# Low parts of projection weights: a ScalarE negation and an accumulating DMA in place of a subtraction

## The chip, the cores and the metric

One core of a Trainium2 chip runs the whole kernel. The metric is the time of one execution on the device in microseconds; a kernel's time is the median over its runs.

## The reference, cut to what matters

The kernel computes a trunk of two layers on 512 tokens of width 1024, all in float32: an S5 state-space mixer, a SwiGLU feed-forward block (FFN), a sparse attention with a lightning indexer (DSA), and a second FFN.

```python
def s5_mixer(u, ..., w_glu):
    ...
    y = jax.nn.gelu(y).astype(u.dtype)
    val, gate = jnp.split(y @ w_glu, 2, axis=-1)      # w_glu: 1024 x 2048
    return val * jax.nn.sigmoid(gate)

def dsa_mixer(h, w_in, q_gain, k_gain, w_o, cos, sin, topk):
    proj = h @ w_in                                   # w_in: 1024 x 3656
    q, k, v, qi, ki, wi = jnp.split(proj, cuts, axis=-1)
    ...                                               # QK-norm, rotary
    # per block of 128 queries
    score = jnp.einsum('bqhk,bqh->bqk', jax.nn.relu(s_idx), wb)   # 8 index heads
    _, sel = lax.top_k(score, topk)                   # 256 keys of each query
    ...                                               # 16 heads attend to the selected keys
    return out @ w_o
```

## The kernel before, in words

Every float32 product with a weight is made of three products in TensorE's faster type fp32r: a weight block w is split into a high part (w rounded to fp32r) and a low part (w minus the high part), the activations are split in the same way, and high x high, high x low and low x high are summed in PSUM (`mm3` L271 to L274 for the mixer and the FFNs, `project` L1016 to L1030 for the attention's projections). `wblock` (L254 to L268) brings a block of up to 128 x 1024 weights in: a DMA on SyncE's queue (SP, L262) fills `w_raw`, ScalarE (ACT) copies it into `w_hi` with rounding (L263), and the low part is subtracted on VectorE (DVE, L265) or, where a caller hands an engine in, on GpSimd (POOL, L267). There are two buffers of `w_raw`, three of `w_hi` and three of `w_lo`.

Who calls it, in the program's order:

- The S5 layer. While VectorE still builds the state-space operators and TensorE runs the scan, `refill` (L815) fetches 11 blocks of `w_glu` of 512 to 1024 columns for partial sums of the GLU projection, with which `glu_parts` fills the gaps of TensorE. After the scan, `glu_sum` (L844) adds what is missing in 16 blocks of 128 to 768 columns. Their low parts come from VectorE.
- The attention. `weights` (L1011) fetches the columns that a projection needs, in two or three blocks, and their low parts come from GpSimd: five blocks for the index heads (`index_heads`), eight for the values (`values`, four head groups) and four per head group for the queries and keys (`queries_keys`, s = 0 to 3), 29 in all. Queries and keys of head group 0, the index scores (`score`, L1119 and L1121 on VectorE), the choice of the 256 keys (`select`, MAX8 L1133 and MATCH_REPLACE L1134 on VectorE) and the values stand before the first attention scores (`scores`, L1203 and L1204); the head groups 1 to 3 are projected while the group before them attends.
- The two FFNs and the output projection take 152 further blocks, with their low parts on VectorE.

GpSimd also does small steps of the norms of heads (`head_norm`, `hn_ms`, `hn_pw` and the factor `kf`, `fk` or `nsq`), memsets and the causal masks. A tile scheduler sets the order of the instructions on every engine from the order in which the kernel is written and from the buffers; each engine runs its own list in order, and semaphores tie the lists together.

Of the kernel before, what the change touches and what calls it, by code (L numbers as in the profile page):

```python
# [15 lines left out]
AF = mybir.ActivationFunctionType  # L16
ALU = mybir.AluOpType
# [3 lines left out]
P = 128  # L21
D = 1024
# [32 lines left out]
HD = 64  # L55
# [150 lines left out]
class Trunk:  # L206
# [47 lines left out]
    def wblock(self, src, nk, cols, lo_engine=None):  # L254

        nc = self.nc
        raw_t = self.wp.tile([P, KT * P], F32, name="w_raw", bufs=2)
        hi_t = self.wp.tile([P, KT * P], F32R, name="w_hi", bufs=3)
        lo_t = self.wp.tile([P, KT * P], F32R, name="w_lo", bufs=3)
        raw, hi, lo = (t[:, : nk * cols] for t in (raw_t, hi_t, lo_t))  # L260
        v = "p (k c) -> p k c"
        nc.sync.dma_start(out=raw.rearrange(v, k=nk), in_=src)  # L262
        nc.scalar.activation(hi, raw, AF.Copy)  # L263
        if lo_engine is None:
            nc.vector.tensor_tensor(lo, raw, hi, op=ALU.subtract)  # L265
        else:
            lo_engine.tensor_tensor(lo, raw, hi, op=ALU.subtract)  # L267
        return hi.rearrange(v, k=nk), lo.rearrange(v, k=nk)  # L268
# [98 lines left out]
    def s5(self, gain_row, x_ap, lre, lim, ldt, b_re, b_im, c_re, c_im, d_ap, w_glu):  # L367
        nc, tc = self.nc, self.tc
        V, PL, AC, PE = nc.vector, nc.gpsimd, nc.scalar, nc.tensor
        ident = self.ident  # L370
        wg = w_glu.rearrange("(k p) f -> p k f", p=P)
# [37 lines left out]
        def load_x(j):  # L409
            for e in range(2):  # L410
# [8 lines left out]
                          in_=gain_row.rearrange("(o d) -> o d", o=1).to_broadcast([P, D]))  # L419
# [383 lines left out]
        cuts = [u for u in range(UN) for _ in range(GLU_BLOCKS[u])]  # L803
        cut.update(zip(order, cuts))
        groups, n = [], 0
        while n < len(order):
            m = n + 1
# [3 lines left out]
            n = m  # L811
# [3 lines left out]
        def refill(ahead):  # L815
            while fetched[0] < min(len(groups), done[0] + ahead):
                n, m = groups[fetched[0]]
                fetched[0] += 1
                d, i = order[m - 1]
                whi, wlo = self.wblock(wg[:, 0 : cuts[n], i * D + d * P : i * D + (d + m - n) * P], cuts[n], (m - n) * P)  # L820
                for b in range(n, m):
                    c = slice((m - 1 - b) * P, (m - b) * P)
                    ready[b] = whi[:, :, c], wlo[:, :, c]
# [18 lines left out]
                yield  # L842

        def glu_sum(d, i, k0, k1):  # L844
            whi, wlo = self.wblock(wg[:, k0:k1, i * D + d * P : i * D + (d + 1) * P], k1 - k0, P)
            pt = self.acc()
            for k in range(k0, k1):
                self.mm3(pt, whi[:, k - k0], wlo[:, k - k0], y[k], k == k0, k == k1 - 1)
            return pt
# [40 lines left out]
        for u in range(UN):  # L890
# [30 lines left out]
            if more:  # L921
                ES[u + 1] = turns_out(u + 1, E[u + 1])
            refill(3 if u else 2)
            filler(GLU_BLOCKS[u] * u - sum(f))
        manual.close()
# [14 lines left out]
        for d in range(KT):  # L940
            ps = []
            for i in (1, 0):
                ps.append(glu_sum(d, i, cut[d, i], KT))
            sg = self.tmp("A", "sg")
            vl = self.tmp("B", "vl")
            V.tensor_tensor(sg, ps[0], part[d][:, 1], op=ALU.add)
            AC.activation(sg, sg, AF.Sigmoid)
            V.tensor_tensor(vl, ps[1], part[d][:, 0], op=ALU.add)
            V.tensor_tensor(vl, vl, sg, op=ALU.mult)
            V.tensor_tensor(self.x[d], self.x[d], vl, op=ALU.add)  # L950
# [14 lines left out]
    def dsa(self, gain, w_in, qg, kg, w_o, rope_ap):  # L965
        nc, tc = self.nc, self.tc
        V, PL, AC, PE = nc.vector, nc.gpsimd, nc.scalar, nc.tensor
        win = w_in.rearrange("(k p) f -> p k f", p=P)
# [10 lines left out]
        for i, g in ((1, qg), (2, kg)):  # L979
            gbt = sp.tile([P, HD], F32, name=f"rope_g{i}")  # L980
            nc.sync.dma_start(out=gbt, in_=g.rearrange("(o d) -> o d", o=1).to_broadcast([P, HD]))
            for dst, src in ((slice(0, HD), slice(0, HD)), (slice(HD, HD + H), slice(H, HD)),
                             (slice(HD + H, 2 * HD), slice(0, H))):
                n = dst.stop - dst.start
# [23 lines left out]
        ki = self.slot("a12", [P, 2, S], "ki", F32R)  # L1008
        PL.memset(ki[HD:, 1].bitcast(F32), 0.0)

        def weights(c0, n):  # L1011
            nk = min(KT, KT * P // n)
            out = []
            for k0 in range(0, KT, nk):
                m = min(nk, KT - k0)
                whi, wlo = self.wblock(win[:, k0 : k0 + m, c0 : c0 + n], m, n, PL)  # L1016
                out += [(whi[:, j], wlo[:, j]) for j in range(m)]
            return out

        def project(w, t, n):  # L1020

            pt = self.acc(proj_bank[0])
            ts = slice(t * P, (t + 1) * P)
            for k, (whi, wlo) in enumerate(w):
                for i, (l, ww) in enumerate(((0, whi), (1, whi), (0, wlo))):
                    PE.matmul(pt[:, :n], lhsT=h[k][:, l, ts], rhs=ww, start=(k == 0 and i == 0),  # L1026
                              stop=(k == KT - 1 and i == 2))
                if k == KT // 2 - 1:
                    yield
            return pt  # L1030
# [8 lines left out]
        def head_norm(src, nh, t, out, scale):  # L1039

            sqv = self.tmp("B", "hn_sq")[:, : nh * HD].rearrange("p (h d) -> p h d", d=HD)
            ms = sp.tile([P, 4], F32, name="hn_ms", bufs=2)
            for i in range(nh):
                AC.activation(sqv[:, i], src[:, i], AF.Square, accum_out=ms[:, i : i + 1])
            PL.tensor_scalar(ms[:, :nh], ms[:, :nh], r2[:, t : t + 1], EPS, op0=ALU.mult, op1=ALU.add)
            pw = sp.tile([P, 4], F32, name="hn_pw", bufs=2)
            PL.tensor_tensor(pw[:, :nh], ms[:, :nh], self.mhalf[:, :nh], op=ALU.pow)
            PL.tensor_scalar(out, pw[:, :nh], rt[:, t : t + 1], scale, op0=ALU.mult, op1=ALU.mult)

        def hv(ap, nh):  # L1050
            return ap[:, : nh * HD].rearrange("p (h d) -> p h d", d=HD)

        def rope(src, tab, t, nh):
            ab = self.tmp("A", "rope_ab")
            ro = sp.tile([P, 4 * HD], F32, name="ro", bufs=3)
            self.rope(hv(ro, nh), src, tab, t, nh, hv(ab, nh), hv(ab[:, S // 2 :], nh))
            return ro
# [81 lines left out]
        def values(s):  # L1139
            w = weights(2 * D + s * 4 * HD, 4 * HD)  # L1140
            for t in range(TB):
                pt = whole(project(w, t, 4 * HD))
                AC.activation(vv[t][:, s * 4 * HD : (s + 1) * 4 * HD], pt[:, : 4 * HD], AF.Copy, scale=rt[:, t : t + 1])
                yield
# [4 lines left out]
        def flush():  # L1149
            while late:  # L1150
                late.pop()()

        def queries_keys(s):

            q, k = ([self.slot(f"a{s % 2 * 5 + 2 * i + e}", [P, 2, S], f"{nm}{s}{e}", F32R) for e in range(2)]
                    for i, nm in enumerate(("q", "k")))
            kl = [self.slot(t, [P, 2, S], f"kl{s}{e}", F32R)
                  for e, t in enumerate((f"a{s % 2 * 5 + 4}", ("a10", "a11", "a12", "a15")[s]))]
            for e in range(2):
                PL.memset(kl[e][half[1 - e]].bitcast(F32), 0.0)  # L1160
            qk[s] = q, k, kl
            for j in range(2 * TB):
                t, isq = j % TB, j // TB
                if t == 0:
                    w = weights((1 - isq) * D + s * 4 * HD, 4 * HD)
                pt = yield from project(w, t, 4 * HD)
                if isq:
                    head_norm(hv(pt, 4), 4, t, nsq[:, t, s * 4 : s * 4 + 4], -(HD**-0.5))
                    ro = rope(hv(pt, 4), qtab, t, 4)
                    nxt = partial(put_q, q, ro, t)  # L1170
                else:
                    fk = sp.tile([P, 4], F32, name="fk", bufs=2)
                    head_norm(hv(pt, 4), 4, t, fk, 1.0)
                    ro = rope(hv(pt, 4), ktab, t, 4)
                    V.tensor_tensor(hv(ro, 4), hv(ro, 4), fk.unsqueeze(2).to_broadcast([P, 4, HD]), op=ALU.mult)
                    nxt = partial(put_k, k, kl, ro, t)
                flush()
                late.append(nxt)
                yield
# [102 lines left out]
        proj_bank = [None]  # L1282
        index_heads()
        mix(queries_keys(0), score(), 2, 3)
        flush()
        mix((None for s in range(4) for _ in values(s)), select(), 1, 3)
# [78 lines left out]
```

## Time and profile before

| | |
|---|---|
| median of 3 runs | 1295.48 us (1294.7 to 1298.88) |
| the profiled execution, its own time | 1299.89 us |
| its span | 1298.2 us |
| mean granted TensorE clock | 0.99 of full speed |
| S5 layer with its GLU | about 0 to 235 us of the span |
| attention up to its first scores | about 590 to 721 us |
| DMA traffic | 108.65 MB, 84 GB/s in the mean |

In the rows below, PE is TensorE's matmuls, PEld its weight loads, DVE VectorE, ACT ScalarE, POOL GpSimd and SP SyncE. Times are microseconds of the profiled execution unless ns is named. A row of the view by stretches gives the stretch, its length and each engine's busy time in it (with the count of instructions), then the granted clock, the busy share of the 16 DMA engines and GB/s.

### The profile page before, as it was taken

How to read it: one execution, taken by the hardware profiler on the slowest of the kernel's cores; microseconds unless marked ns; L12 is line 12 of the kernel's file. 1: busy time of each engine (PE TensorE's matmuls, PEld its weight loads, DVE VectorE, ACT ScalarE, POOL GpSimd, SP SyncE). 2: the span in 40 equal slices, each digit the busy share in tenths (PEclk: the TensorE clock that was granted, in tenths of full speed). 3: DMA queues.
4: the chain of work that ended last, by engine and by line, in shares of the span. 5: the costliest groups of instructions: out<-in, count | busy, mean ns of one | idle time of the engine just before them, and what ended most of it. 6: DMA issues, size and time to landing. Idle time of an engine off the chain costs nothing.

```text
span 1298.2 us, 17961 instructions
## 1 busy us (share of the span) xinstructions
PE 1223.8 (94%) x6796; PEld 1048.7 (81%) x6796; DVE 769.0 (59%) x1546; ACT 541.9 (42%) x1224; POOL 150.5 (12%) x177
## 2 busy tenths in 40 slices
PE   2569999999999999999989799999999999999998
PEld 1457878888888888888989799998888888888887
DVE  7999958654444443335899977775754444443221
ACT  5645536433333322223563678875533333332221
POOL 2000000000000000005744354520000000000000
PEclk9979999999999999999999899999999999999999
DMA  5101223333333333332213111111333333333341
GB/s 139 54 19 52 71 84 114 104 98 97 97 98 98 98 92 99 94 105 71 92 52 98 49 50 34 42 30 53 106 112 95 96 96 95 97 93 101 108 118 46
DMA packets 189894, 108.65 MB, mean 84 GB/s; under 512 B 7224, under 2 KB 188560, under 8 KB 189744
## 3 DMA queue, kind: packets, MB, share of 16 engines
q1 hardware_dynamic: 189424, 107.35, 28.4%
q8 instruction: 53, 0.87, 0.3%
q14 instruction: 33, 0.27, 0.1%
q10 hardware_dynamic: 384, 0.16, 0.1%
HBM read 103.04 MB, written 2.10 MB: 81 GB/s over the span
## 4 chain that ended last, share of the span: by engine, by line
PE 75%; DVE 8%; ACT 1%; issue 1%; DMA 0%; POOL 0%; ACTq 0%; DVEq 0%; POOLq 0%
PE acc L272 21%; PE acc L273 21%; PE acc L274 21%; PE acc L1026 7%; PE acc L1231 2%; DVE mask L1134 2%; DVE m L1133 2%; PE tr L1220 1%; DVE mask L1121 1%; PE lg L1204 1%; DVE pe L1207 1%; PE lg L1203 1%; PE tr L1063 0%; DVE kl L1081 0%; ACT pe L1210 0%
## 5 line engine op out<-in xcount | busy, mean ns | idle before, releaser
L263 ACT ACTIVATE w_hi<-w_raw 128x1024 fp32r<-128x1024 f32 (+5 forms) x208 | 199.9, 963 | 508.2 <-PE acc L273 461.1
L265 DVE TENSOR_TENSOR w_lo<-w_raw,w_hi 128x1024 fp32r<-128x1024 f32 (+6 forms) x179 | 194.2, 1085 | 146.5 <-ACT w_hi L263 145.4
L272 PE MATMUL acc<-h,w_hi 128*128 128x512 f32 x704 | 274.5, 390 | 0.0
L274 PE MATMUL acc<-h,w_lo 128*128 128x512 f32 x704 | 273.9, 389 | 0.0
L273 PE MATMUL acc<-h,w_hi 128*128 128x512 f32 x704 | 273.7, 389 | 0.0
L1026 PE MATMUL acc<-w_hi,h 128*128 128x256 f32 (+1 forms) x896 | 175.6, 293 | 0.8 <-ACT h L284 0.8
L272 PEld LDWEIGHTS acc<-h,w_hi 128*128 128x128 f32 x704 | 132.1, 188 | 28.0 <-issue 0.5
L274 PEld LDWEIGHTS acc<-h,w_lo 128*128 128x128 f32 x704 | 132.1, 188 | 27.6
L273 PEld LDWEIGHTS acc<-h,w_hi 128*128 128x128 f32 x704 | 132.1, 188 | 27.5 <-issue 0.5
L1026 PEld LDWEIGHTS acc<-w_hi,h 128*128 128x128 f32 x896 | 142.1, 193 | 1.4 <-ACT h L284 1.0
L1026 PE MATMUL acc<-w_lo,h 128*128 128x256 f32 (+1 forms) x448 | 127.3, 289 | 0.3 <-POOL w_lo L267 0.3
L339 DVE TENSOR_TENSOR u<-acc,rinv 128x512 f32<-128x512 f32 x44 | 30.4, 691 | 132.4 <-PE acc L274 132.4
L272 PE MATMUL acc<-f,w_hi 128*128 128x512 f32 x272 | 106.4, 391 | 0.0
L274 PE MATMUL acc<-f,w_lo 128*128 128x512 f32 x272 | 105.9, 389 | 0.0
L273 PE MATMUL acc<-f,w_hi 128*128 128x512 f32 x272 | 105.8, 389 | 0.0
L1026 PEld LDWEIGHTS acc<-w_lo,h 128*128 128x128 f32 x448 | 85.5, 193 | 0.8 <-POOL w_lo L267 0.5
L336 DVE TENSOR_TENSOR g<-acc,rinv 128x512 f32<-128x512 f32 x44 | 30.4, 691 | 85.3 <-PE acc L274 85.1
L267 POOL TENSOR_TENSOR w_lo<-w_raw,w_hi 128x1024 fp32r<-128x1024 f32 (+2 forms) x29 | 69.5, 2407 | 47.6 <-ACT w_hi L263 46.8
L274 PEld LDWEIGHTS acc<-f,w_lo 128*128 128x128 f32 x272 | 51.0, 188 | 10.8
L273 PEld LDWEIGHTS acc<-f,w_hi 128*128 128x128 f32 x272 | 51.1, 188 | 10.4
L272 PEld LDWEIGHTS acc<-f,w_hi 128*128 128x128 f32 x272 | 51.1, 188 | 10.4
L272 PE MATMUL acc<-y,w_hi 128*128 128x512 f32 x128 | 51.9, 414 | 1.7 <-ACT y L796 1.1
(288 smaller groups left out, 1979.4 us busy)
## 6 DMA issues: line engine op xcount, KB each, us to landing
w_raw<-in_ffn_w_gate_up_dram SPq DMA_DIRECT2D x88, 512.0 KB, 3.7
w_raw<-in_ffn_w_down_dram SPq DMA_DIRECT2D x32, 448.0 KB, 3.5
w_raw<-in_dsa_w_in_dram SPq DMA_DIRECT2D x26, 512.0 KB, 3.4
w_raw<-in_ffn_w_down_dram SPq DMA_DIRECT2D x16, 512.0 KB, 3.7
w_raw<-in_dsa_w_o_dram SPq DMA_DIRECT2D x16, 256.0 KB, 2.9
w_raw<-in_s_w_glu_dram SPq DMA_DIRECT2D x6, 384.0 KB, 3.3
xc<-in_x_dram SPq DMA_DIRECT2D x8, 256.0 KB, 8.9
xr<-in_x_dram SPq DMA_DIRECT2D x4, 512.0 KB, 3.7
```

The costliest lines, as they stand in the source:

```text
L263: nc.scalar.activation(hi, raw, AF.Copy)
L265: nc.vector.tensor_tensor(lo, raw, hi, op=ALU.subtract)
L267: lo_engine.tensor_tensor(lo, raw, hi, op=ALU.subtract)
L272: mm(out, lhsT=whi, rhs=xx[:, 0], start=start, stop=False)
L273: mm(out, lhsT=whi, rhs=xx[:, 1], start=False, stop=False)
L274: mm(out, lhsT=wlo, rhs=xx[:, 0], start=False, stop=stop)
L336: nc.vector.tensor_tensor(g, ps[0], rinv, op=ALU.mult)
L339: nc.vector.tensor_tensor(u, ps[1], rinv, op=ALU.mult)
L1026: PE.matmul(pt[:, :n], lhsT=h[k][:, l, ts], rhs=ww, start=(k == 0 and i == 0), stop=(k == KT - 1 and i == 2))
L1133: V.max(m8, sc)
L1134: V.match_replace(out=sc, in_to_replace=m8, in_values=sc, imm_value=GONE)
L1231: PE.matmul(po[s, b][:, i * HD : (i + 1) * HD], lhsT=pT[:, j * P : (j + 1) * P], rhs=vv[j][:, (s * 4 + i) * HD : (s * 4 + i + 1) * HD], st ...
```

## The change

A third way to make the low part. With `"dma"` in the place of the engine, ScalarE writes minus the high part into `w_lo`, and a DMA from GpSimd's queue reads the weights a second time from HBM and adds them to it. `refill`, `glu_sum`, the index heads, the values and the queries and keys of head group 0 take it: 27 blocks whose low parts were VectorE's, and 17 that were GpSimd's. The 12 blocks of the head groups 1 to 3 stay on GpSimd, those of the FFNs and of the output projection on VectorE. Lines behind L264 have three more in the changed kernel.

```diff
@@ wblock
         nc.sync.dma_start(out=raw.rearrange(v, k=nk), in_=src)
         nc.scalar.activation(hi, raw, AF.Copy)
-        if lo_engine is None:
+        if lo_engine == "dma":
+            nc.scalar.activation(lo, hi, AF.Copy, scale=-1.0)
+            nc.gpsimd.dma_start(out=lo.rearrange(v, k=nk), in_=src, accum_op=ALU.add)
+        elif lo_engine is None:
             nc.vector.tensor_tensor(lo, raw, hi, op=ALU.subtract)
@@ refill
-                whi, wlo = self.wblock(wg[:, 0 : cuts[n], i * D + d * P : i * D + (d + m - n) * P], cuts[n], (m - n) * P)
+                whi, wlo = self.wblock(wg[:, 0 : cuts[n], i * D + d * P : i * D + (d + m - n) * P], cuts[n], (m - n) * P, "dma")
@@ glu_sum
-            whi, wlo = self.wblock(wg[:, k0:k1, i * D + d * P : i * D + (d + 1) * P], k1 - k0, P)
+            whi, wlo = self.wblock(wg[:, k0:k1, i * D + d * P : i * D + (d + 1) * P], k1 - k0, P, "dma")
@@ dsa
-        def weights(c0, n):
+        def weights(c0, n, lo="dma"):
...
-                whi, wlo = self.wblock(win[:, k0 : k0 + m, c0 : c0 + n], m, n, PL)
+                whi, wlo = self.wblock(win[:, k0 : k0 + m, c0 : c0 + n], m, n, lo)
@@ queries_keys
-                    w = weights((1 - isq) * D + s * 4 * HD, 4 * HD)
+                    w = weights((1 - isq) * D + s * 4 * HD, 4 * HD, PL if s else "dma")
```

The scheduler moves instructions with it. GpSimd's list between the last index heads and the first keys of head group 0, before (`hn_ms`, `hn_pw` and `kf`, `fk` are the steps of the head norms, `kl` a low part of the keys, cleared):

```order
L1048 TENSOR_SCALAR kf<-hn_pw,rt 128x1
L267 TENSOR_TENSOR w_lo<-w_raw,w_hi 128x1024 x2
L1045 TENSOR_SCALAR hn_ms<-hn_ms,r_4748 128x1
L1160 MEMSET kl_7849 64x1024
L1047 TENSOR_TENSOR hn_pw<-hn_ms,mhalf 128x1
L267 TENSOR_TENSOR w_lo<-w_raw,w_hi 128x1024
L1048 TENSOR_SCALAR kf<-hn_pw,rt 128x1
L1045 TENSOR_SCALAR hn_ms<-hn_ms,r_4748 128x4
```

And there in the changed kernel:

```order
L1051 TENSOR_SCALAR kf<-hn_pw,rt 128x1
L266 DMA w_lo<-in_dsa_w_in_dram 128x4x256 x2
L1048 TENSOR_SCALAR hn_ms<-hn_ms,r_4775 128x1
L1050 TENSOR_TENSOR hn_pw<-hn_ms,mhalf 128x1
L1051 TENSOR_SCALAR kf<-hn_pw,rt 128x1
L1163 MEMSET kl_7893 64x1024
L1048 TENSOR_SCALAR hn_ms<-hn_ms,r_4775 128x4
```

The subtractions are gone from GpSimd's list; in their place stand the issues of two DMAs, ahead of the same small steps.

TensorE's list in the values of head group 2, before (`w_hi_6052` and `w_lo_6053` are the first block of the pair, `w_hi_6058` and `w_lo_6059` the second, `acc1_6063` the sum of the first 128 tokens, `acc1_6133` that of the third):

```order
L1026 MATMUL acc1_6133<-w_lo_6053,h1_4676 128x256
L1026 MATMUL acc1_6133<-w_hi_6052,h2_4682 128x256 x2
L1026 MATMUL acc1_6133<-w_lo_6053,h2_4682 128x256
L1026 MATMUL acc1_6133<-w_hi_6052,h3_4688 128x256 x2
L1026 MATMUL acc1_6063<-w_lo_6059,h4_4694 128x256
L1026 MATMUL acc1_6063<-w_hi_6058,h5_4700 128x256 x2
L1026 MATMUL acc1_6063<-w_lo_6059,h5_4700 128x256
```

And in the changed kernel (first block `w_hi_6092` and `w_lo_6093`, second `w_hi_6099` and `w_lo_6100`; `acc1_6105` belongs to the first tokens, `acc0_6211` to the fourth; L1206 and L1207 are the first attention scores):

```order
L1029 MATMUL acc0_6211<-w_lo_6093,h3_4715 128x256
L1029 MATMUL acc0_6211<-w_hi_6099,h4_4721 128x256 x2
L1206 MATMUL lg_6403<-k00_5203,q00_5201 128x128
L1207 MATMUL lg_6403<-kl00_5205,q00_5201 128x128
L1206 MATMUL lg_6412<-k01_5204,q01_5202 128x128
L1029 MATMUL acc1_6105<-w_lo_6100,h4_4721 128x256
L1029 MATMUL acc1_6105<-w_hi_6099,h5_4727 128x256 x2
```

Before, the low part of the second block is first used when the first block has served not quite three of the four groups of tokens; now it is when it has served all four, and the first attention scores, which stood behind the values of all head groups, stand there too.

ScalarE's list at the start of the GLU sums, before (`xk` are the transposed inputs, `sg` the gate):

```order
L938 ACTIVATE xk_1956<-tr 128x512
L263 ACTIVATE w_hi<-w_raw 128x256
L263 ACTIVATE w_hi<-w_raw 128x384
L947 ACT_TABLE_LOAD
L947 ACTIVATE sg<-sg 128x512
L938 ACTIVATE xk_1963<-tr 128x512
```

And in the changed kernel:

```order
L941 ACTIVATE xk_1967<-tr 128x512
L263 ACTIVATE w_hi<-w_raw 128x256
L263 ACTIVATE w_hi<-w_raw 128x384
L265 ACTIVATE w_lo<-w_hi 128x256
L950 ACT_TABLE_LOAD
L950 ACTIVATE sg<-sg 128x512
L265 ACTIVATE w_lo<-w_hi 128x384
L941 ACTIVATE xk_1974<-tr 128x512
```

The negation of a block stands behind its high part, sometimes with other work of ScalarE between the two.

## Rows read from the trace of the kernel before

**Rows 1.** The page: engines' busy times and shares; the chain by engine.

```profile
PE 1223.8 (94%) x6796; PEld 1048.7 (81%) x6796; DVE 769.0 (59%) x1546; ACT 541.9 (42%) x1224; POOL 150.5 (12%) x177
...
PE 75%; DVE 8%; ACT 1%; issue 1%; DMA 0%; POOL 0%; ACTq 0%; DVEq 0%; POOLq 0%
```

**Rows 2.** Stretches: S5 layer, GLU sums, attention up to its first scores.

```profile
0.00:50.00 50.00, 16.34 (x107) 13.87 (x107) 40.32 (x187) 33.87 (x85) 7.46 (x17) 1.00 0.43 110
50.00:100.00 50.00, 34.58 (x282) 28.78 (x282) 49.26 (x96) 21.82 (x52) 0.23 (x2) 0.86 0.11 29
100.00:150.00 50.00, 48.23 (x346) 39.45 (x347) 47.74 (x87) 24.65 (x51) 0.34 (x3) 1.00 0.21 57
200.00:255.00 55.00, 55.00 (x253) 45.46 (x252) 42.48 (x66) 27.71 (x43) 1.93 (x1) 1.00 0.40 117
...
640.00:755.00 115.00, 102.01 (x777) 98.46 (x776) 110.61 (x279) 66.11 (x214) 57.90 (x53) 0.96 0.21 65
644.00:721.00 77.00, 68.92 (x529) 66.92 (x528) 74.53 (x170) 40.51 (x113) 41.21 (x32) 0.96 0.24 76
...
645.00:655.00 10.00, 7.39 (x55) 7.01 (x54) 9.77 (x18) 5.82 (x29) 6.28 (x7) 0.95 0.35 107
```

**Rows 3.** Timeline from 644 to 653 us, in part, of POOL, DVE and PE.

```profile
644.07 4.94 POOL L267 TENSOR_TENSOR w_lo<-w_raw,w_hi 128x1024 fp32r<-128x1024 f32 x2
644.46 2.29 DVE L963 TENSOR_TENSOR ro<-rope_ab 128x256 f32<-128x256 f32 x1
646.67 2.62 DVE L1121 SCALAR_TENSOR_TENSOR mask<-pe,wi,mask 128x256 f32<-128x256 f32 x1
649.10 0.57 POOL L1045 TENSOR_SCALAR hn_ms<-hn_ms,r 128x4 f32<-128x4 f32 x1
...
652.86 0.41 PE L1063 MATMUL tr<-ident,ro 128*128 128x128 f32 x2 [2.51 <-DVE kl L1081]
```

**Rows 4.** VectorE's groups, 630 to 720 us, then single lines: ns min/median/max.

```profile
L1121 DVE SCALAR_TENSOR_TENSOR mask<-pe,wi,mask 128x256 f32<-128x256 f32 (+2 forms) x21 | 18.8, 897 | 0.2
L963 DVE TENSOR_TENSOR ro<-rope_ab 128x256 f32<-128x256 f32 (+1 forms) x10 | 9.7, 969 | 0.2
...
L1121 DVE SCALAR_TENSOR_TENSOR mask<-pe,wi,mask x21: 469/619/2617, 637.0 to 688.0; 128x256 f32<-128x256 f32 x7, 128x384 f32<-128x384 f32 x7, 128x512 f32<-128x512 f32 x7
...
L963 DVE TENSOR_TENSOR ro<-rope_ab x10: 226/422/2622, 629.3 to 670.9; 128x256 f32<-128x256 f32 x9, 128x64 f32<-128x64 f32 x1
...
L1136 DVE TENSOR_SCALAR mask<-mask x3: 349/428/2343, 692.8 to 755.1; 128x256 f32<-128x256 f32 x1, 128x384 f32<-128x384 f32 x1, 128x512 f32<-128x512 f32 x1
...
L1119 DVE TENSOR_SCALAR mask<-pe,wi x3: 411/479/1743, 635.2 to 673.3; 128x256 f32<-128x256 f32 x1, 128x384 f32<-128x384 f32 x1, 128x512 f32<-128x512 f32 x1
```

**Rows 5.** The chain that ended last, 640 to 725 us, in part.

```profile
682.32 2.57 DVE mask L1121
...
692.90 2.26 DVE mask L1136
```

**Rows 6.** VectorE's low parts in the S5 layer: three up to 100 us, first and last.

```profile
37.81 0.69 DVE L265 TENSOR_TENSOR w_lo<-w_raw,w_hi 128x512 fp32r<-128x512 f32 x1 [0.80 <-ACT w_hi L263]
...
48.41 0.95 DVE L265 TENSOR_TENSOR w_lo<-w_raw,w_hi 128x768 fp32r<-128x768 f32 x1
```

**Rows 7.** ScalarE's high parts by shape, 30 to 260 us: busy us, mean ns.

```profile
L263 ACT ACTIVATE w_hi<-w_raw 128x1024 fp32r<-128x1024 f32 x8 | 8.4, 1057 | 16.1 <-PE acc L273 10.2 <-DMA w_raw<-in_ffn_w_gate_up_dram 5.9
...
L263 ACT ACTIVATE w_hi<-w_raw 128x640 fp32r<-128x640 f32 x6 | 4.4, 738 | 6.4 <-DMA w_raw<-in_s_w_glu_dram 3.6 <-PE acc L273 2.9
```

**Rows 8.** DMA issues: count, KB each, median us from issue to landing.

```profile
w_raw<-in_dsa_w_in_dram SPq DMA_DIRECT2D x26, 512.0 KB, 3.4
...
w_raw<-in_s_w_glu_dram SPq DMA_DIRECT2D x5, 256.0 KB, 2.6
```

**Rows 9.** VectorE's low parts of the last twelve GLU sums, first and last.

```profile
198.59 0.55 DVE L265 TENSOR_TENSOR w_lo<-w_raw,w_hi 128x384 fp32r<-128x384 f32 x1
...
227.91 0.95 DVE L265 TENSOR_TENSOR w_lo<-w_raw,w_hi 128x768 fp32r<-128x768 f32 x1
```

## The prediction

> **What bounds the kernel now.** I read the page first. TensorE is busy 94% of the span and the chain of waits is 75% TensorE, 8% VectorE [rows 1]. So an instruction taken from another engine counts only where TensorE waits, and I looked for those places with the view by stretches. There are two that the change touches.
>
> In the S5 layer VectorE builds operators and is busy for 49.26 of the 50 us from 50 to 100, while TensorE idles 15.4; from 100 on TensorE is busy for 48.23 of 50, and over the GLU sums for all of it [rows 2]. In the attention, from 644 to 721 us, VectorE is busy for 74.53 of 77 us, TensorE idles 8.1 and its clock is granted at 0.96, which takes 68.92 x 0.04 = 2.8 more; over the wider stretch from 640 to 755 it idles 13.0 and loses 4.1 at the same clock [rows 2]. The first score of the attention waits there for VectorE's choice of keys.
>
> The timeline shows why VectorE is late in the second place. While GpSimd subtracts two low parts (4.94 us), a VectorE sum of two SBUF tiles takes 2.29 us and the next instruction, with two such inputs as well, 2.62; TensorE then stands for 2.51 until VectorE gives it `kl` [rows 3]. The same lines take 0.42 and 0.62 in the median [rows 4]. Against the medians the 21 L1121 lose 21 x (0.897 - 0.619) = 5.8 us, the ten L963 10 x (0.969 - 0.422) = 5.5, the first L1136 2.34 - 0.35 = 2.0 and the first L1119 1.74 - 0.48 = 1.3: 14.6 us between 630 and 720. Two of these stand in the chain itself, with 2.57 and 2.26 us [rows 5]. Some 11.6 of the 14.6 start behind 644, seven instructions from the 2.29 at 644.46 to the 2.26 at 692.90.
>
> **The change part by part.**
>
> *S5 layer, VectorE's 27 subtractions go.* Only three stand where TensorE idles, 0.69, 0.95 and 0.95 us at 37.8 to 49.4 [rows 6]; the other 24 run while TensorE is saturated and are worth nothing. That is 2.6 us off a VectorE that sets the pace there. Bounds 0 and 4 (the clock, 0.86 in that stretch, could come up sooner); I take **-2.5**.
>
> *Attention, 17 of GpSimd's subtractions go* (17 of the 19 up to 721 us). VectorE gets its 14.6 us back. It can turn into time only up to what TensorE waits: 8.1 + 2.8 = 10.9 us from 644 to 721, and 17.1 to 755. The 3 us before 644 and part of the wait that is one of TensorE's own order bring nothing. Below, 4 (what stands in the chain: 2.57 - 0.75 and 2.26 - 0.35); above, 14. I take **-8**, two thirds of the waits: VectorE is 97% busy, so nearly all of the 11.6 shifts its later work, and the first scores now stand ahead of the last values, which gives TensorE something to do during the choice of keys.
>
> *ScalarE negates 44 blocks*, at 1.06 us for 1024 columns and 0.74 for 640 [rows 7], 17 x 1.0 + 27 x 0.7 = 36 us in all. It is busy for 40.51 of 77 and 27.71 of 55 us in those stretches [rows 2], so this lies beside other work; what it costs is lateness of the low part, counted next.
>
> *44 accumulating DMAs.* No row shows one. Below, it costs what a plain load costs, 3.4 us for 512 KB and 2.6 for 256 [rows 8]; above, three of them in a row (read the weights, read the tile, write it), 10.2 and 8.6 for the 288 KB of a mean GLU block (at some 2.85 each). Two 512 KB blocks take a share of 0.35 of 16 engines over 10 us [rows 2], so one pass takes 1.75. I take a load, one pass more and an issue of GpSimd like its small steps (0.57 [rows 3]): 3.4 + 1.75 + 0.6, rounded to 6 us, and 2.85 + 1.0 + 0.6 = 4.5 for the GLU. By a sentence of its own: the Trainium skill, "DMA: Bandwidth & Descriptors", section "Anatomy of one DMA — SWDGE (gpsimd) path", fits a plain DMA of GpSimd's queue as 2.0 us plus its bytes over 436e3 per us, an estimate of 3.2 for 512 KB; by it the low part would be earlier than I count, and the trace has no such DMA.
>
> Does TensorE wait for them? A buffer of `w_lo` is held from ScalarE's write to TensorE's last use, and there are three. In the GLU sums the last twelve blocks [rows 9] have 576 columns in the mean, 13.5 matmuls at 55.00/253 = 0.217 us [rows 2], 2.9 us of TensorE each. High part 0.7, negation 0.7, DMA t, use 2.9: three buffers keep pace if 4.3 + t is at most 3 x 2.9, so up to **t = 4.4**. At 4.5 the stall is nothing, at 8.6 it is (4.3 + 8.6)/3 - 2.9 = 1.4 per block, 17 us over twelve. In the attention a block serves 48 matmuls of some 0.12 us, 5.8 us, and 1.05 + 1.05 + t + 5.8 within 17.4 allows up to t = 9.5; the new order of TensorE's list, all four groups of tokens on the first block of a pair, covers one such block. The 11 blocks of the partial sums are spread over 100 us. I take **+1.5** for starts (the first index heads, the first GLU sums), bounds 0 and 21.
>
> *GpSimd's queue.* The small steps of the head norms stand behind DMAs that wait for ScalarE; before, they stood behind 4.9 us of subtractions, so nothing is added. *SyncE* issues the same loads; `w_raw` comes free after ScalarE instead of after the subtraction, 2.4 us sooner, hidden. *HBM* carries the weights of 44 blocks twice, some 16 MB; DMA shares of 0.24 and 0.40 [rows 2] leave room.
>
> Sum: -2.5 - 8 + 1.5 = **-9**. The profiled execution took 1299.89, so it would take 1290.9; it stands 4.4 above the median of the runs, 1295.48, on which the forecast is **1286.5**.
>
> **The rivals.**
>
> *The low parts come late* (slower). An accumulating DMA really takes three passes one after another. It decides at t = 4.4 us in the GLU sums: at 8.6 TensorE loses 17 there. In the attention at 10.2 the cycle is 18.1 against 17.4, 0.2 for each of 17 blocks, 4 in all, and the late values and queries give back half of the 8. 1295.5 + 17 + 4 - 4 - 1 is some **1311**; at t = 7 in the GLU, (4.3 + 7)/3 - 2.9 = 0.9, 10 us, and some **1300**. For it: no row shows such a DMA, and the GLU has the shortest blocks. Against it: the engines are idle for more than half of the time.
>
> *VectorE's gain is hidden* (same). TensorE's waits from 644 to 721 come from its own order (its list places a projection behind transposes that need VectorE's whole rotary chain), so the gain is the 4 us of the chain, the S5 part moves into TensorE's next wait, and 2 to 3 us of late low parts cancel it: **1294**.
>
> *GpSimd still holds VectorE* (faster by less). GpSimd's instruction and VectorE's exclude each other for their whole length [rows 3]. If GpSimd's issue of a DMA needs the same lock, it waits for VectorE's instructions of 0.4 to 1 us, and holds VectorE for its own 1 us or so in place of 2.4: the 8 shrinks to 5, t rises by 0.5 to 1 and the GLU loses 2 to 4. **1292**. The rule behind it is in the Trainium skill, "SBUF — State Buffer", section "SBUF: two separate sides": while VectorE runs in a mode that takes both port pairs, GpSimd can't write the descriptors of its DMAs. That page's section "Who interferes with whom" also says that a VectorE instruction with two SBUF inputs contends with a GpSimd one that reads SBUF; the trace agrees, 2.62 against 0.62 us in the median. No run here shows the descriptors' part.
>
> *More than forecast.* VectorE's start in the S5 layer pulls the clock up and all 17.1 us of waits up to 755 shrink by 14: **1278**.
>
> *It doesn't do what it says.* The order of instructions has the 44 DMAs and no such subtraction; I give it nothing.
>
> **How the numbers follow.** Forecast as it stands 0.44, more than forecast 0.08, GpSimd still in the way 0.12, hidden 0.14, late low parts 0.22. About 0.3%, 3.9 us, is what a measurement of this kernel can tell from no change, so faster means below 1291.6 and slower above 1299.4. The forecast, the best case and half of the third, which lies on the bound, are faster by more: 0.58. The other half and the hidden case, but for 0.02 of it, are the same: 0.18. The late low parts and those 0.02 are slower: 0.24. The range runs from 1277 (4 and 14 gained with no stall, the best case with it) through the hidden case to the middle of the late one, 1305; the far half of that one and the tails, under 0.2, are left out.
>
> **What would show it.** Right: from 640 to 700 no L1121, L963 or L1136 over 1 us; VectorE's last choice of keys before the first score some 10 us sooner; TensorE's idle time from 644 to 721 below 4 us; its waits for `w_lo` under 3 us in all; accumulating DMAs of 4 to 6 us from issue to landing. Wrong: waits of TensorE for `w_lo` of 1 us or more at each GLU sum, DMAs of 8 us and more, or VectorE still at 2 us with GpSimd free of subtractions. The stretch from 100 to 180 us and all behind the attention's first scores should keep their lengths.

## The result and the profile after

The changed kernel takes **1328.76 us** in the median of 4 runs (1324.74 to 1330.8), the one before 1296.26 beside it: 1.0245 times as long, 95% interval 1.0215 to 1.0275. The profiled execution took 1328.88 us, its span is 1327.0. The forecast was 1286.5, in a range from 1277 to 1305.

The page of the changed kernel: its engines and its chain by engine, then the DMA queues with packets, MB and share of 16 engines, and three kinds of DMA issues.

```profile
PE 1235.9 (93%) x6796; PEld 1058.2 (80%) x6796; DVE 732.6 (55%) x1519; ACT 576.1 (43%) x1268; POOL 166.5 (13%) x204
...
q1 hardware_dynamic: 189424, 107.35, 27.9%
q0 software_dynamic: 23232, 17.07, 9.3%
...
PE 76%; DMA 6%; DVE 6%; issue 4%; ACT 4%; POOL 1%; SPq 1%; ACTq 0%; POOLq 0%; DVEq 0%
...
w_raw<-in_dsa_w_in_dram SPq DMA_DIRECT2D x26, 512.0 KB, 3.5
w_lo<-in_dsa_w_in_dram POOLq DMA_DIRECT2D x14, 512.0 KB, 7.3
...
w_lo<-in_s_w_glu_dram POOLq DMA_DIRECT2D x6, 384.0 KB, 6.6
```

VectorE is busy for 36.4 us less and ScalarE for 34.2 more [rows 1]; the prediction had counted 36 more for ScalarE. New is that DMA stands in the chain with 6%, where it had none, and that the new queue moves 17.07 MB: a 512 KB accumulation lands 7.3 us after its issue, where a load of the same size takes 3.5.

Where the time went is read from the first and last starts of a few lines in both traces, which cut the span into stages (us):

| stage | before | after | difference |
|---|---|---|---|
| start to the first transposes of the inputs (the scan is done) | 192.8 | 190.4 | -2.4 |
| from there to the last GLU matmul | 45.0 | 62.0 | **+17.0** |
| first FFN, from its first matmul to the first projection | 360.9 | 360.9 | 0.0 |
| first projection to the last attention matmul | 306.4 | 320.5 | **+14.1** |
| the rest | 392.9 | 393.0 | +0.1 |

The five differences add up to 28.8 us, not to the 32.5 of the medians, because the profiled execution of the kernel before was itself 3.6 us above its median. Both losses lie where low parts come by DMA. TensorE's waits in the stretch of the GLU sums, then in the attention, after (line waited for, total us, times, longest):

```profile
PE acc L277 <- DMA w_lo<-in_s_w_glu_dram: 10.3, 5, 3.6
PE tr L940 <- ACT xk L941: 1.4, 1, 1.4
...
PE acc L1029 <- DMA w_lo<-in_dsa_w_in_dram: 17.0, 6, 5.3
```

Before, TensorE's matmuls waited 0.2 us in the GLU sums, and 0.3 for GpSimd's low parts in the attention. How one wait comes about is shown by rows of the GLU sums after: first ScalarE's rows for a block of 640 columns and for the block three later, which takes over its buffer, then GpSimd's issue of the DMA, the chain, and TensorE's row:

```profile
211.70 0.74 ACT L263 ACTIVATE w_hi<-w_raw 128x640 fp32r<-128x640 f32 x1 [1.21 <-PE acc L276]
212.47 0.74 ACT L265 ACTIVATE w_lo<-w_hi 128x640 fp32r<-128x640 f32 x1
...
226.39 0.74 ACT L263 ACTIVATE w_hi<-w_raw 128x640 fp32r<-128x640 f32 x1 [6.64 <-PE acc L276]
...
213.50 1.51 POOL L266 DMA_DIRECT2D w_lo<-in_s_w_glu_dram  x1 [1.43 <-ACT w_lo L265]
...
213.50 8.21 DMA w_lo<-in_s_w_glu_dram
221.75 6.43 issue
...
221.76 0.50 PE L277 MATMUL acc<-y,w_lo 128*128 128x512 f32 x1 [3.63 <-DMA w_lo<-in_s_w_glu_dram]
```

ScalarE starts the high part at 211.70, GpSimd issues the DMA at 213.50, it lands at 221.71, and TensorE, which has waited 3.63 us for it, goes on at 221.76. Ten microseconds, for a block that gives TensorE 3.3 us of work. Meanwhile ScalarE sits 6.64 us until TensorE gives the buffer back, and the next round begins late. The waits are 12 of the 17 us. TensorE is also busy for longer, 50.27 us (190 to 252.6) against 44.81 before (193 to 238): behind this wait and behind one of 3.05 us its granted clock is 0.50, the lower of its two levels, from 223.2 to 226.1 and from 240.5 to 243.2 us, and its matmuls start 0.43 us apart there and not 0.23. That is some 2.8 us of the 17.

In the attention the chain that ended last passes through six of these DMAs, 45 us in all:

```profile
611.17 8.14 DMA w_lo<-in_dsa_w_in_dram
...
630.63 8.24 DMA w_lo<-in_dsa_w_in_dram
...
651.33 8.03 DMA w_lo<-in_dsa_w_in_dram
...
670.29 7.62 DMA w_lo<-in_dsa_w_in_dram
...
691.42 5.79 DMA w_lo<-in_dsa_w_in_dram
...
721.09 7.41 DMA w_lo<-in_dsa_w_in_dram
```

What the change was for did happen. VectorE's index scores in the attention, after, ns min/median/max, to be held against [rows 4]:

```profile
L1124 DVE SCALAR_TENSOR_TENSOR mask<-pe,wi,mask x21: 466/611/751, 668.5 to 718.5; 128x256 f32<-128x256 f32 x7, 128x384 f32<-128x384 f32 x7, 128x512 f32<-128x512 f32 x7
```

The longest takes 0.75 us, no longer 2.62. From 644 to 721 us, 30 to 107 us behind the first projection, VectorE is busy for 56.90 us; in the kernel before it was 73.83 at the same distance (629.4 to 706.4 us). But the last MATCH_REPLACE of the choice of keys comes 167.5 us behind the first projection, before 155.0.

### The profile page after: what moved, and what is told of

The parts are those of the page before. It is cut to its first block, busy times and chain, and to the rows that moved or that the text cites. A ratio compares the mean times of both kernels' runs of the same rounds, so it can differ in the third digit from the quotient of the medians.

```text
span 1327.0 us, 18064 instructions
## 1 busy us (share of the span) xinstructions
PE 1235.9 (93%) x6796; PEld 1058.2 (80%) x6796; DVE 732.6 (55%) x1519; ACT 576.1 (43%) x1268; POOL 166.5 (13%) x204
## 3 DMA queue, kind: packets, MB, share of 16 engines
q1 hardware_dynamic: 189424, 107.35, 27.9%
q0 software_dynamic: 23232, 17.07, 9.3%
## 4 chain that ended last, share of the span: by engine, by line
PE 76%; DMA 6%; DVE 6%; issue 4%; ACT 4%; POOL 1%; SPq 1%; ACTq 0%; POOLq 0%; DVEq 0%
PE acc L275 20%; PE acc L276 20%; PE acc L277 20%; PE acc L1029 7%; DMA w_lo<-in_dsa_w_in_dram 3%; PE acc L1234 2%; DMA w_lo<-in_s_w_glu_dram 1%; PE tr L1223 1%; PE acc L780 1%; PE acc L781 1%; POOL w_lo L266 1%; SPq L688 1%; DMA craw<-in_s_c_re_dram 1%; ACT xn L582 1%; DMA M<-Kd 1%
## 5 line engine op out<-in xcount | busy, mean ns | idle before, releaser
L268 DVE TENSOR_TENSOR w_lo<-w_raw,w_hi 128x1024 fp32r<-128x1024 f32 (+2 forms) x152 | 172.9, 1138 | 130.2 <-ACT w_hi L263 128.9
L277 PE MATMUL acc<-y,w_lo 128*128 128x512 f32 x128 | 52.0, 407 | 10.6 <-DMA w_lo<-in_s_w_glu_dram 10.3
L277 PEld LDWEIGHTS acc<-f,w_lo 128*128 128x128 f32 x272 | 51.0, 188 | 10.8
L276 PEld LDWEIGHTS acc<-f,w_hi 128*128 128x128 f32 x272 | 51.1, 188 | 10.3
```

Of the source, the lines that this page charges most:

```text
L276: mm(out, lhsT=whi, rhs=xx[:, 1], start=False, stop=False)
L277: mm(out, lhsT=wlo, rhs=xx[:, 0], start=False, stop=stop)
```

## The experiments

Ratios are to the kernel before, timed beside each experiment on the same chip; the experiment without a ratio was executed once.

**The parts by themselves.** Two of the three places go back to their subtractions:

```diff
-    ... (m - n) * P, "dma")                          # refill
+    ... (m - n) * P)
-    ... k1 - k0, P, "dma")                           # glu_sum
+    ... k1 - k0, P)
-        def weights(c0, n, lo="dma"):                # the attention, with queries_keys
+        def weights(c0, n, lo=PL):
```

Partial sums alone:

> Only the 11 blocks of the GLU partial sums have their low part from negation and accumulating DMA. In the changed kernel the scan's last transposes came 2.4 us sooner (190.2 against 192.6 us). Late-low-part theory: this part alone gains 2 to 3 us, so 1293 to 1294.5. Rival (the second read of the weights loads the DMA engines and delays everything on them): no gain or a loss, 1296 to 1300.

1296.93 us, ratio 1.0008 (0.9999 to 1.0017): nothing gained. The gain is in the trace, and something that takes it back. TensorE's waits from 36 to 195 us, first before, then with this part (its lines are three higher):

```profile
PE tr L647 <- ACT WT L648: 5.3, 1, 5.3
PE tr L647 <- DVE W L636: 4.7, 1, 4.7
...
PE acc L777 <- DMA M<-Kd: 1.8, 1, 1.8
```

```profile
PE acc L780 <- DMA M<-Kd: 5.7, 3, 3.1
...
PE tr L650 <- ACT WT L651: 1.0, 1, 1.0
PE tr L650 <- DVE W L642: 0.9, 1, 0.9
```

TensorE's waits for VectorE's tables `W` and their turned copies `WT` shrink by 8 us, but the small copies `M<-Kd` between tiles of SBUF now share the DMA engines with the accumulations (56 KB land in 3.8 us, before in 2.0; 48 KB in 4.5 against 2.0), and TensorE waits for those, 5.7 us instead of 1.8. Its wait for VectorE's `X` grows too, from 1.1 to 3.6 us.

GLU sums alone:

> Only the 16 blocks of the GLU sums. From the scan's last transposes to the last GLU matmul the changed kernel took 62.2 us where the one before took 45.2. If the loss belongs to these blocks alone: 1296 + 17, so 1311 to 1315, and TensorE's waits for w_lo some 10 us there. If it came from the partial sums' DMAs running into them: clearly less, under 1305.

1308.1 us, 1.009 (1.0069 to 1.0112), 11.9 us. Their stage takes 54.7 us, 9.7 more than before; beside the partial sums' DMAs it was 17.0 more. So neither expectation held: 7 of the 17 us come only in the company of the other parts. Why is not shown; the stage differs by TensorE's wait for `w_lo`, 5.4 us here against 10.3, and by its granted clock, 1.00 here against 0.95.

Attention alone:

> Only the 17 blocks of the attention up to its scores. The changed kernel took 320.5 us from the first projection to the last attention matmul, the one before 306.4. Late-low-part theory: 1296 + 14, so 1307 to 1313, with VectorE's L1121 and L963 at their medians (no instruction over 0.8 us) and TensorE waiting 15 us and more for w_lo. If VectorE's relief were worth the forecast 8 us and the loss came from elsewhere: under 1292.

1313.06 us, 1.0127 (1.0104 to 1.015), 16.9 us; its stage takes 320.1. TensorE waits there 15.9 us for `w_lo`, and no L1121 is over 0.75 us. The three parts together make 29.5 of the 32.5 us.

**The negation without the DMA.**

```diff
             nc.scalar.activation(lo, hi, AF.Copy, scale=-1.0)
-            nc.gpsimd.dma_start(out=lo.rearrange(v, k=nk), in_=src, accum_op=ALU.add)
+            (nc.gpsimd if add_pl else nc.vector).tensor_tensor(lo, lo, raw, op=ALU.add)
```

> As the changed kernel, ScalarE's negation of all 44 blocks too, but VectorE (GLU) or GpSimd (attention) adds w_raw to it instead of the accumulating DMA. If ScalarE's 36 us of negations in its list cost the time: 1310 or more. If the DMA does (late-low-part theory and the traffic theory alike): 1296 to 1301, a low part later by about 1 us only.

1299.84 us, 1.0029 (1.0019 to 1.0039). ScalarE's 44 negations with an addition by an engine cost 3.7 us, not 30 (the GLU sums' stage takes 47.7 us): the DMA is the loss.

**Lateness or traffic.** More buffers, in tiles that are free in these stages:

```diff
+        if spare is None:
             hi_t = self.wp.tile([P, KT * P], F32R, name="w_hi", bufs=3)
             lo_t = self.wp.tile([P, KT * P], F32R, name="w_lo", bufs=3)
+        else:
+            hi_t = self.slot(spare[0], [P, KT * P], "w_hx", F32R)
+            lo_t = self.slot(spare[1], [P, KT * P], "w_lx", F32R)
...
+  glu_sum: spare = ("a12", "a13") for every fourth block
+  weights: spare = {3: ("a5", "a6"), 4: ("a7", "a8")}.get(n_blk[0] % 5)
```

> The changed kernel with more buffers for high and low parts: every fourth block of the GLU sums, and two of every five blocks of the attention, take theirs from tiles that are free in these stages. Late-low-part theory (a low part is late by its own latency, which three buffers don't cover): with four buffers the cycle of a GLU block is (1.4 + 8 + 2.9)/4 = 3.1 against 2.9 us, so most of the 17 us of the GLU sums go, and with five in the attention most of its 14 and some of VectorE's relief shows: 1290 to 1305. Traffic theory (the DMA engines, busy for 0.85 of the GLU sums, set the pace): 1322 to 1330 as before.

1303.67 us, 1.0056 (1.0036 to 1.0077): 25 of the 32.5 us are back, with every byte of the traffic still there. The GLU stage takes 51.2 us, counted to the last matmul with the additional tiles, and has 10.8 of its 17.0 us back; the attention takes 307.8 us and has 12.7 of its 14.1 back. And the traffic without the wait:

```diff
             whi, wlo = self.wblock(wg[:, k0:k1, i * D + d * P : i * D + (d + 1) * P], k1 - k0, P)
+            nc.gpsimd.dma_start(out=dst, in_=wg[:, k0:k1, i * D + d * P : i * D + (d + 1) * P], accum_op=ALU.add)
```

(`dst` is one of two tiles that nobody reads.)

> The kernel before, with 16 accumulating DMAs of the GLU sums' weights into two tiles that nobody reads; low parts by VectorE as before. It is the traffic without the wait. Late-low-part theory: 1296 to 1300. Traffic theory: 1304 to 1312, w_raw landing in 4 us and more.

1299.31 us, 1.0023 (1.0013 to 1.0032). The DMA engines are as busy as in the changed kernel, here from 200 to 255 us in this run, then in the changed kernel:

```profile
200.00:255.00 55.00, 53.96 (x246) 44.00 (x246) 41.55 (x62) 27.91 (x43) 15.49 (x12) 1.00 0.81 159
```

```profile
200.00:255.00 55.00, 44.45 (x177) 34.17 (x176) 26.39 (x39) 28.31 (x45) 15.40 (x11) 0.94 0.85 156
```

A DMA share of 0.81 against 0.85 and 159 against 156 GB/s, but TensorE is busy for 53.96 of 55 us and not for 44.45. The traffic of the GLU sums costs the kernel 3 us (their stage takes 46.5 us, 1.5 more than before); the lateness costs the rest. The traffic of the attention was not run by itself; there the version with more buffers, which carries all of it, speaks for the lateness.

**What the DMA's time is made of.**

```diff
-            nc.gpsimd.dma_start(out=lo.rearrange(v, k=nk), in_=src, accum_op=ALU.add)
+            nc.gpsimd.dma_start(out=lo, in_=raw, accum_op=ALU.add)
```

> The changed kernel, with the accumulating DMA reading w_raw in SBUF and not HBM a second time. A look at the DMA's own time: in the changed kernel it is 7.3 us from issue to landing for 512 KB. If the read from HBM makes it so: 5 us or less. If reading and writing the tile that it adds to does: 7 us again.

Its page:

```profile
q0 software_dynamic: 6336, 17.07, 7.3%
...
w_lo<-w_raw POOLq DMA_DIRECT2D x16, 512.0 KB, 4.8
```

4.8 us for 512 KB: 2.5 of the 7.3 us go when the DMA reads SBUF. Whether that is HBM or the number of packets stays open, since the edit also takes the packets from 23232 to 6336. It doesn't help, since `w_raw` is held until the DMA has landed: SyncE's loads wait 218.7 us for `w_lo`, ScalarE waits 47 us for the `w_raw` of the attention and of the GLU projection (in the changed kernel no such wait has a row of more than 0.4), and the one execution took 1331.02 us.

**What VectorE's relief is worth.** First without GpSimd and without a DMA, the 17 blocks subtracted on VectorE (`weights(c0, n, lo=None)`):

> The kernel before, with the 17 blocks of the attention up to its scores subtracted on VectorE in place of GpSimd: 17 x 1.1 = 19 us more of VectorE's own work, but no GpSimd instruction that holds it (14.6 us). If VectorE's busy time sets the pace there: 1298 to 1304. If what counted were low parts that come in time, 1.1 us instead of 2.4: 1290 to 1296.

1299.35 us, 1.0021 (1.0011 to 1.0032). This can't tell the relief from the 17 us of subtractions that VectorE takes on. Then with the DMA where fewer low parts need to be late: index heads on VectorE, values and head group 0 by DMA, with two of every five blocks in additional tiles.

```diff
-            w = weights(q0, 4 * HD)                   # both calls in index_heads
+            w = weights(q0, 4 * HD, None)
```

> Low parts of the S5 layer by VectorE as before. In the attention the five blocks of the index heads are subtracted on VectorE, the twelve of the values and of head group 0 take negation and accumulating DMA, with two of every five in tiles that are free there (more buffers). Theory: with enough buffers what is left of the loss is that the index heads' first low parts come late, and VectorE's choice of keys starts 6 us later (60.7 against 54.9 us behind the first projection). Without that, VectorE's relief shows: 1287 to 1293. Rival: the relief is worth nothing, since TensorE has the work anyway: 1296 to 1299.

1297.42 us, 1.0007 (0.9997 to 1.0016). With the index heads on GpSimd:

> The same, with the index heads' five blocks on GpSimd as before. Some of the instructions that GpSimd holds (629 and 635 us in the trace before) stay. Theory: 1289 to 1295, a little behind the version with VectorE. Rival: 1296 to 1299.

1298.22 us, 1.0015 (1.0005 to 1.0024). The tiles without any DMA:

> The kernel before, with the same additional tiles for two of every five of these 17 blocks, low parts by GpSimd. It shows what the tiles alone are worth. Theory (TensorE waited 0.8 us in all for GpSimd's low parts): 1294 to 1298.

1294.73 us, 0.9985 (0.9974 to 0.9996). The run with the index heads on VectorE still had a stall of 5 us, so its first three blocks, and then three of every six, got tiles of their own (`{1: ("a5", "a6"), 2: ("a7", "a8"), 3: ("a9", "a11")}.get(n_blk[0] % 6)`), and, in two further runs, blocks of head group 0 went to VectorE:

> Index heads on VectorE; values and head group 0 by negation and DMA, as in the run with the index heads on VectorE, but with three additional pairs of tiles, and the first three blocks in them. In that run TensorE lost 5 us and its clock fell to 0.74 at 620 to 640 us, because the first such low part was asked for only at 624.9 us, when the index heads gave a buffer back. If VectorE's relief is worth something once no low part is late: 8 to 9 us under that run, 1287 to 1291. If TensorE has its work anyway and the stall only takes up its slack: 1294 to 1297.

1298.58 us, 1.0012 (1.0 to 1.0023).

> The same with the two blocks of head group 0's keys on VectorE too, so that the first low part by DMA is needed 12 us later. If lateness at the start is all that is left: as good as or better than the run with early tiles, 1287 to 1292. If VectorE's own time counts as much: 1293 to 1297.

1300.32 us, 1.0033 (1.002 to 1.0045).

> The same with all four blocks of head group 0 on VectorE, only the eight of the values by DMA. If VectorE's own 9 subtractions (10 us) there cost as much as GpSimd's held it: 1294 to 1298. If the values' blocks, on which VectorE stood in the chain at 682 and 692 us, are what counts: 1288 to 1292.

1298.61 us, 1.002 (1.0011 to 1.003). All three lie above both of the times expected. So with lateness nearly gone (one wait of 2.5 us for a low part with early tiles, none worth a row with the values alone) the relief brings nothing. The stretches of the run with early tiles, then those before (the view adds up the times of packets, so its DMA share can pass 1):

```profile
620.00:640.00 20.00, 17.17 (x133) 16.46 (x132) 12.28 (x45) 14.54 (x53) 13.96 (x24) 1.00 1.18 234
640.00:660.00 20.00, 19.50 (x159) 19.09 (x158) 15.21 (x42) 16.99 (x62) 12.44 (x19) 1.00 0.81 171
```

```profile
620.00:640.00 20.00, 19.75 (x152) 19.24 (x151) 17.09 (x48) 11.78 (x50) 15.29 (x21) 1.00 0.27 81
640.00:660.00 20.00, 17.39 (x127) 17.01 (x126) 19.58 (x46) 14.30 (x63) 15.38 (x17) 0.91 0.18 54
```

VectorE is busy for 27.5 of these 40 us where it was 36.7: the time it no longer loses to GpSimd it spends idle. From 600 to 700 us it waits 7.9 us for ScalarE's squares of the projections (`hn_sq`) and 2.6 for the projections themselves; before, it waited 2.9 for the projections and for no squares. Its choice of keys then takes 6 us less (first to last MATCH_REPLACE 62.1 to 155.9 us behind the first projection, before 54.9 to 155.0), but begins 7 later. In TensorE's list of that version the last index score stands behind 575 matmuls of projections, in the list before behind 488. The first attention matmul with the values does come sooner, 123.8 us behind the first projection with early tiles and 119.4 with the values alone, before 127.6; the last one doesn't (308.3 and 306.7, before 306.4). TensorE waits there 6.7 and 8.5 us for VectorE's masking of the scores (`nm`), where it waited 3.7.

That left the order as the suspect. TensorE's list over head group 0 and the index scores was kept as the kernel is written:

```diff
+        with tc.manual_schedule(engines={mybir.EngineType.PE}):
-        mix(queries_keys(0), score(), 2, 3)
-        flush()
+            mix(queries_keys(0), score(), 2, 3)
+            flush()
```

> The kernel before, with TensorE's list over head group 0 and the index scores kept as written instead of the scheduler's: the last index score then stands behind 429 matmuls of projections, not 488. Order theory (the start and end of VectorE's choice of keys follow from where the index scores stand in TensorE's list): the choice ends sooner, 1288 to 1295, unless TensorE then waits for the rotary chain, which GpSimd's instructions make late (1296 to 1302).

1300.21 us, 1.0031 (1.002 to 1.0043).

> The run with early tiles (index heads on VectorE, values and head group 0 by DMA), with TensorE's list kept as written there too: the last index score behind 448 matmuls of projections; it was behind 575 in that run. Order theory: VectorE's relief shows now, since the list no longer puts projections ahead of the scores: 8 us and more under that run's 1298.6, so 1284 to 1291. Rival (the relief is worth nothing in any order): 1296 to 1300.

1306.15 us, 1.0079 (1.0062 to 1.0096).

> The run with the values' blocks alone by DMA, and TensorE's list kept as written over head group 0 and the index scores, last score behind 448 matmuls. Order theory: 1286 to 1293. Rival: 1296 to 1300.

1303.65 us, 1.0055 (1.004 to 1.007). The choice of keys does end sooner, 141.3, 143.8 and 146.8 us behind the first projection instead of 155.0, and still not sooner with the DMA than without; and TensorE now waits for ScalarE to take the index scores out of PSUM (6.9, 7.4 and 10.1 us), since the projections that filled those gaps stand elsewhere. All three are slower than the same kernel in the scheduler's order. The order theory falls with these runs: the relief is worth nothing in either order.

**A version that beats both.** More tiles and no DMA:

> The kernel before with additional tiles for three of every six of the attention's 17 blocks, low parts by GpSimd, no DMA: a version meant to beat both. With two of five it took 0.9985 of the time before (0.9974 to 0.9996). If more tiles ahead are worth more: 1291 to 1294. If what that gained was the order of TensorE's list and not the tiles: 1295 to 1298.

1298.86 us, 1.0021 (1.0012 to 1.0031). None was found that beats the kernel before by more than the 0.3% that a measurement tells; what the tiles gained with two of five was within that, and with three of six it was gone.

## Why the prediction was wrong

1. **VectorE's 27 subtractions, -2.5.** Measured alone: 0 (1.0008). The relief was there, 8 us fewer waits for VectorE's tables; the step that failed is the one that DMA shares "leave room", which looked at the mean share and not at the small copies `M<-Kd` in the same engines, whose time doubled. The stage's -2.4 in the changed kernel's trace can't be set against that: kernels whose S5 layer is that of the kernel before show 188.8 to 192.9 us there.

2. **ScalarE's negations beside other work, 0.** Nearly right: 3.7 us with the addition on an engine.

3. **The DMA's price, t = 6 and 4.5.** Mis-sized low: 7.3 for 512 KB, and in the GLU sums 4.8 for 256 KB, 7.1 for 320, 8.0 for 384 in the medians of that stretch, 8.2 and 8.4 for the two in the chain. A load and one pass of 1.75 more was too little, and no row had the 2.85 for a load of 288 KB (the rows have 2.6 for 256 KB and 3.4 for 512); by the queues' rows the accumulation takes 9.3/17.07 against 27.9/107.35 of a share per MB, 2.1 times the engines' time of a load. The Trainium skill, "DMA: Bandwidth & Descriptors", section "Anatomy of one DMA — SWDGE (gpsimd) path", would have had an estimate of 3.2 us by its fit of 2.0 us plus bytes over 436e3; the trace has 7.3 for the accumulating kind, which the fit isn't said to be for.

4. **The cycle of three buffers in the GLU sums, +0 of the 1.5.** The bound was right in kind, t up to 4.4, and the DMA lies beyond it. It was still too friendly: it put 1.4 us between the start of the high part and the issue, and the timeline has 1.6 to 2.5 for the last blocks and up to 4.7 where other work of ScalarE stands between. The stage lost 17.0 us, which is what the rival "the low parts come late" gave for t = 8.6, but that agreement is luck. With the 6.1 us that t was in the mean of the last twelve blocks, the prediction's sum gives 7 us, and 9 with 2.0 us from the high part to the issue; the GLU sums alone lost 9.7. The other 7 are in part the lower clock behind the long waits (2.8), and the rest is not explained. That the larger part of the loss is lateness for want of a buffer, and not the traffic, is shown by the run with a fourth buffer (10.8 of the 17.0 us back) and by the traffic alone (3 us).

5. **The cycle in the attention, +0 to 1.** Here the step failed that let a buffer serve 5.8 us. It rests on the first block of a pair being done with all four groups of tokens before the second begins, and the place of TensorE's list that stands ahead of the prediction, in head group 2, was not the rule. In the values of head group 1, and of head group 3 in the same way, the list runs through both blocks for one group of tokens before it goes to the next:

```order
L1029 MATMUL acc1_5950<-w_lo_5945,h7_4739 128x256
L1029 MATMUL acc0_5985<-w_lo_5938,h0_4699 128x256
L1029 MATMUL acc0_5985<-w_hi_5937,h1_4703 128x256 x2
```

   `w_lo_5945` belongs to the second block, `w_lo_5938` to the first, and that one is needed until the last group. Both are held for nearly all of the pair's 11.5 us, and (2.1 + 7.3 + 11.5)/3 = 7.0 us against 5.8 is an estimated loss of 1.2 for such a block. In the changed kernel's list 8 of the 17 blocks are held for two thirds of their pair's matmuls or more, so this makes some 10 us of the 14.1 that the stage lost; the rest is not accounted for. Two further pairs of buffers brought the loss to 1.4 us, which shows that buffers were what was missing.

6. **VectorE's relief in the attention, -8.** The largest term, and worth nothing. "VectorE is 97% busy, so nearly all of the 11.6 shifts its later work" took busy time for work: without the stretching VectorE waits for the projections and for ScalarE's squares of them, as the run with early tiles shows. Of the stretched instructions three stood in the chain, the two of [rows 5] and an L963 of 2.06 us at 663.62, and even the 4 us of those two, the lower bound of the term, did not come. In the six runs on VectorE's relief in the scheduler's order the choice of keys ended 154.9 to 158.0 us behind the first projection, before 155.0; with more buffers and all 17 blocks by DMA it was 153.7. Where it ended 8 to 14 us sooner, with TensorE's list kept as written, the kernel was no faster either, because TensorE lost the time among the index scores. "Hidden", which the rivals gave 0.14, was right for this term, though not for the reason given there. Shown is that the relief has no value in these two orders of TensorE's list with the low parts by DMA; with them on VectorE its own added work hides what it is worth, and whether an order exists in which it has a value stays open.

7. **GpSimd still in the way.** This rival falls: with 17 issues of 1.3 us on GpSimd no L1121 (L1124 in the changed kernel) is over 0.75 us. The Trainium skill, "SBUF — State Buffer", section "Who interferes with whom", says that a VectorE instruction with two SBUF inputs contends with a GpSimd one that reads SBUF, not with one that only writes it; the trace agrees as far as it goes, 2.62 us at most beside GpSimd's subtractions before, 0.75 beside its issues after. That VectorE holds up the writing of descriptors is neither shown nor excluded here.

So the sign followed the rival that had 0.22. Its price of +17 for the GLU sums was met, by luck in its size; its +4 for the attention was 14 to 17; and the gains that it set against them did not exist. The steps of the forecast that failed are the DMA's t, the 5.8 us for which a buffer was said to serve, and the -8 for VectorE's relief: +1.5 for starts stood where 31 us of late low parts were measured, and -10.5 of gains where none was.

## What to carry to other kernels

A step that makes an operand later was paid here in buffers far more than in bandwidth: add up what a buffer goes through (the wait for its release, each writer, the DMA from issue to landing, and the whole time that the consumer's list keeps it, read over all places in the list), divide by the buffers, and compare with the consumer's time for a block. Do this with the shortest blocks, and with a DMA that does not yet stand in the trace at its upper bound. And before an engine's stretched instructions are booked as a gain, look whether it would only wait for someone else in the time that they fill: a busy share of 97% doesn't tell.

## What the runs showed of the hardware

- A 512 KB accumulating DMA from GpSimd's queue lands 7.3 us after its issue when it reads HBM and 4.8 when it reads SBUF in fewer packets, beside 3.5 for a plain load by SyncE; its issue keeps GpSimd for 1.3 us (0.86 from SBUF).
- Small copies by another queue pay for it: 48 KB between tiles of SBUF took 4.5 us beside the accumulations, 2.0 without.
- The accumulations alone, at a DMA share of 0.81 with TensorE reading weights all the time, cost the kernel 3 us only.
- Behind a wait of 3.6 us TensorE's matmuls first stood 0.23 us apart, then 0.43 from 223.2 to 226.1 us, at a granted clock of 0.50, then 0.23 again; the granted clock over the 55 us was 0.94, before 1.00.
